# Four instead of eight output tiles of the heads' projection cut along the depth, and fewer PSUM banks for scores and transposes

## The chip, the core and the metric

The kernel runs on one core of one Trainium2 chip. The metric is the device time of one execution, in microseconds; several runs are given by their median. The engines are PE (TensorE, with its weight loads as PEld), DVE (VectorE), ACT (ScalarE), POOL (GpSimd) and SP, which issues the DMAs.

## What is computed

The program is two blocks of two layers each on a sequence of 512 tokens of width 1024. The first block is not touched. In the second block each layer computes, in the terms of the reference:

```python
y_pool = pool_mixer(u, pool_w, pool_scale)
y_nsa = nsa_mixer(q, kv[:, :, 0], kv[:, :, 1], gates, q_norm, k_norm, cmp_pe, cmp_w1, cmp_w2)
mix = jnp.concatenate([y_pool, y_nsa], axis=-1) @ w_out
x = x + gate1 * mix
h2 = rms_norm(x, norm2) * (1.0 + scale2) + shift2
ff = jnp.square(jax.nn.relu(h2 @ w_ff1)) @ w_ff2
return x + gate2 * ff
```

`nsa_mixer` has eight heads of width 64, each with two masked softmax attentions over the 512 tokens and one over compressed tokens. Rows 512 to 1023 of `w_out` belong to the heads; this product is "the heads' projection".

## The kernel before

Activations lie transposed, 128 features by 512 tokens to a tile; x is eight such tiles, m = 0 to 7. Each operand of a matmul is split into a high and a low part, and `mm3` (line 406 issues each matmul) multiplies high by high, high by low and low by high. A weight "unit" is 512 KB: one DMA into `wraw`, a rounding on ACT into `wH` (line 452) and a subtraction on DVE into `wL` (line 453); three units fit at a time (`wH2`, `wL2`).

In the second block `main2` makes the projections of a layer, and `weave` steps the heads (`nsa_prep`, `nsa`), the compressed attention and the pooling between them. `nsa` runs 16 steps, eight heads with two attentions b = 0, 1 each. A step has two stages, and `two_stage` runs the second stage of one step beside the first of the next:

- first stage, four row blocks of 128 queries: scores on PE into a tile S of PSUM; line 710 on DVE reads S, adds the mask, takes the smallest of the negated scores and writes `p` to SBUF; line 711 on ACT takes the exponential with its sum. Then lines 1759 and 1760 (DVE) make the factors, and line 1764 (POOL, blocks of 128 and 256) and 1766 (DVE, blocks of 384 and 512) scale `p`.
- second stage, four column blocks: transposes on PE (line 415) into a tile M of PSUM, a rounding on ACT (line 419) and a subtraction on DVE (line 420) which both read M; then the product with the values, accumulated over both attentions of a head in one tile M that stays open until line 1792 (ACT) and line 1794 (DVE) have read it. After each second head a 128-wide tile of `yn` is split by lines 419 and 420.

The heads' projection contracts over the four tiles k of `yn`. A matmul result is accumulated in a tile of PSUM and added into x by line 1507 on DVE. Before, the depth is cut in two: a unit `o2h` holds k = 0, 1 or k = 2, 3 of four output tiles. After the flag `yn1` (heads 0 to 3 done) `quad_unit` adds k = 0, 1 of all eight x tiles; after `yn` it adds k = 2, 3 of tiles 0 to 3, and `in_halves` makes a generator that `turn` runs later for k = 2, 3 of tiles 4 to 7, first for tokens 0 to 255, then for tokens 256 to 511. `turn` also makes the sum of squares (lines 650 to 661), its norm (`stat_half`: line 657 adds, ones-matmuls, a power on POOL, a broadcast by matmul) for each half, and `h2` (lines 1347 to 1349), whose result feeds the first three units of the feed-forward product.

The order of all instructions on each engine is not written by hand: a list scheduler places them, and each takes its turn when its operands and a buffer are there. PSUM has eight banks of 128x512 f32, and every PSUM tile takes one. `CAPS` gives for each tag how many tiles may be open at once: in the second block S2 (scores) 3, M2 (all else of the attention) 5, accn2 (projections beside the heads) 2, acc2 (those of `turn` and of the projections before) 7; the eight banks are shared among them.

## Time and profile before

| | |
|---|---|
| median of three runs | 2393.4 us (2393.25 to 2394.74) |
| the profiled execution's own time | 2391.33 us |
| its span | 2389.5 us |
| busy: PE, DVE, ACT, POOL | 98%, 69%, 44%, 11% |
| granted clock of TensorE, mean | 0.994 of 2.4 GHz |

A busy time is the union of an engine's instructions; matmuls are pipelined, so that PE counts as busy also when it could issue faster. The second block's heads run from about 1304 to 1419 us of the span in its first layer, and from 1898 to 2012 us in its second. The windows view gives busy times of a stretch, the timeline gives each instruction, and the waits say what ended an engine's idle time.

### The profile page before, as it was taken

Reading aid. Unit: us, or ns where it says so; the run is one execution under the profiler, and the core shown is the slowest. Engines: PE = TensorE matmul, PEld = TensorE weight load, DVE = VectorE, ACT = ScalarE, POOL = GpSimd, SP = SyncE. Lnnn points to the kernel's source line nnn. Section 1 sums busy time; section 2 is a strip of 40 time slices with the busy share of each in tenths; the row PEclk is TensorE's granted clock in tenths of the full one; section 3 lists DMA queues with packets and bytes.
Section 4 is the critical chain, followed back from the end, with each engine's and each line's share of the span. In section 5 each row is a group of like instructions: output and inputs, shape, how many; then the busy total and the mean of one; then the engine's idle time right before and its main releaser. Section 6 shows DMA issues by size and latency. Waiting matters only on the chain.

```text
span 2389.5 us, 31476 instructions
## 1 busy us (share of the span) xinstructions
PE 2342.3 (98%) x11684; PEld 1973.3 (83%) x11684; DVE 1640.2 (69%) x3410; ACT 1048.7 (44%) x1930; POOL 264.3 (11%) x254
## 2 busy tenths in 40 slices
PE   8999999999999999999999989999999998999999
PEld 7888888888888888888888778888888876888888
DVE  5679975567588987656579886666647988644342
ACT  6455543434446554343246654332324665433231
POOL 0011010000001001000055310000005531000000
PEclk9999999999999999999999999999999999999999
DMA  5222222245543222225332013555523211223222
GB/s 173 88 80 71 80 80 97 82 156 205 182 159 115 71 80 80 97 88 172 126 102 80 27 37 104 193 194 194 193 97 105 68 35 37 80 94 100 98 93 84
DMA packets 87851, 256.62 MB, mean 107 GB/s; under 512 B 9745, under 2 KB 10769, under 8 KB 87697
## 3 DMA queue, kind: packets, MB, share of 16 engines
q1 hardware_dynamic: 87552, 254.45, 31.9%
q8 instruction: 92, 1.51, 0.3%
q14 instruction: 63, 0.51, 0.1%
q10 hardware_dynamic: 144, 0.15, 0.0%
HBM read 250.37 MB, written 4.19 MB: 107 GB/s over the span
## 4 chain that ended last, share of the span: by engine, by line
PE 93%; DVE 5%; ACT 1%; issue 1%; DMA 0%; POOL 0%; DVEq 0%; ACTq 0%; POOLq 0%
PE acc L406 78%; PE M L406 5%; PE accn L406 4%; PE S L406 3%; PE M L415 3%; DVE p L420 1%; DVE p L710 1%; DVE b L1507 1%; DVE wL L453 1%; ACT p L419 0%; DVE p L1766 0%; ACT p L711 0%; DVE tmp_s L1794 0%; DMA wraw<-wp_in 0%; ACT tmp_s L1792 0%
## 5 line engine op out<-in xcount | busy, mean ns | idle before, releaser
L406 PE MATMUL acc<-h,wH 128*128 128x512 f32 (+2 forms) x2944 | 872.6, 380 | 9.5 <-ACT h L423 7.3
L452 ACT CAST wH<-wraw 128x1024 fp32r<-128x1024 f32 x358 | 375.2, 1051 | 656.8 <-PE acc L406 400.0
L406 PEld LDWEIGHTS acc<-h,wH 128*128 128x128 f32 (+1 forms) x2944 | 537.4, 189 | 106.1 <-ACT h L423 7.3
L453 DVE TENSOR_TENSOR wL<-wraw,wH 128x1024 fp32r<-128x1024 f32 x358 | 437.5, 1223 | 164.9 <-ACT wH L452 156.9
L406 PE MATMUL acc<-h,wL 128*128 128x512 f32 (+1 forms) x1440 | 546.2, 380 | 0.0
L406 PE MATMUL acc<-b,wH 128*128 128x512 f32 (+1 forms) x1696 | 503.9, 374 | 0.0
L406 PEld LDWEIGHTS acc<-b,wH 128*128 128x128 f32 x1696 | 311.8, 189 | 56.3
L406 PEld LDWEIGHTS acc<-h,wL 128*128 128x128 f32 x1440 | 272.7, 190 | 49.6
L406 PE MATMUL acc<-wH,h 128*128 128x512 f32 (+1 forms) x1024 | 310.0, 380 | 0.0
L406 PE MATMUL acc<-b,wL 128*128 128x512 f32 (+1 forms) x784 | 291.5, 372 | 0.0
L406 PEld LDWEIGHTS acc<-wH,h 128*128 128x128 f32 x1024 | 187.2, 188 | 33.7
L406 PE MATMUL acc<-wL,h 128*128 128x512 f32 (+1 forms) x512 | 194.7, 380 | 0.0
L1390 DVE SCALAR_TENSOR_TENSOR b<-acc,keep,b 128x512 f32<-128x512 f32 (+1 forms) x68 | 48.9, 720 | 183.9 <-PE acc L406 183.5
L406 PEld LDWEIGHTS acc<-b,wL 128*128 128x128 f32 x784 | 147.9, 189 | 25.4
L711 ACT ACTIVATE p<-p,nb 128x128 f32<-128x128 f32 x192 | 107.9, 564 | 77.7 <-DVE nb L710 76.7
L1325 DVE SCALAR_TENSOR_TENSOR keep<-keep 128x512 f32<-128x512 f32 x192 | 126.0, 686 | 11.1 <-DMA keep<-w_mod_in 10.9
L578 POOL TENSOR_TENSOR sm_bs<-sm_as,keep 128x4 f32<-128x4 f32 (+1 forms) x48 | 65.7, 1376 | 413.4 <-DVE sm_as L574 374.1
L406 PEld LDWEIGHTS acc<-wL,h 128*128 128x128 f32 x512 | 96.5, 188 | 16.2
L406 PE MATMUL S<-b,b 128*128 128x128 f32 (+3 forms) x480 | 108.9, 338 | 0.1
L710 DVE CUSTOM_DVE_ANT_0 p<-S,keep 128x128 f32<-128x128 f32 x192 | 101.3, 542 | 4.9 <-PE S L406 3.6
L415 PE MATMUL M<-keep,p 128*128 128x128 f32 x608 | 97.4, 275 | 2.7 <-DVE tmp_s L1794 1.0
L406 PE MATMUL M<-p,b 128*128 128x256 f32 (+3 forms) x352 | 81.7, 323 | 10.3 <-DVE p L420 9.0
(294 smaller groups left out, 2898.8 us busy)
## 6 DMA issues: line engine op xcount, KB each, us to landing
wraw<-wp_in SPq DMA_DIRECT2D x364, 512.0 KB, 3.5
keep<-w_mod_in SPq DMA_DIRECT2D x192, 256.0 KB, 3.6
b<-x_in SPq DMA_DIRECT2D x8, 256.0 KB, 6.3
g<-x_in SPq DMA_DIRECT2D x8, 256.0 KB, 4.4
x_spill<-tmp_m SPq DMA_DIRECT2D x8, 256.0 KB, 3.9
g<-x_spill SPq DMA_DIRECT2D x8, 256.0 KB, 3.8
out<-b SPq DMA_DIRECT2D x6, 256.0 KB, 2.0
keep<-parq_in SPq DMA_DIRECT2D x2, 384.0 KB, 6.9
```

Of the source, the lines that this page charges most:

```text
L406: return self.nc.tensor.matmul(out, l, r, start=start, stop=stop)
L415: self.nc.tensor.transpose(out, in_, self.ident[:n, :n])
L420: return self.nc.vector.tensor_sub(l, src, fbits(h))
L452: self.cut_h = nc.scalar.copy(h, raw)
L453: self.cut = nc.vector.tensor_sub(l, raw, fbits(h))
L578: self.pow = nc.gpsimd.tensor_tensor(r[:p, :n], m[:p, :n], self.mhalf[:p, :n], ALU.pow)
L710: nc.vector.tensor_tensor_reduce(p, s, mask, nscale, 3e38, ALU.add, ALU.min, accum_out=nb)
L711: nc.scalar.activation(p, p, AF.Exp, bias=nb, scale=-1.0, accum_out=accum)
L1325: nc.vector.scalar_tensor_tensor(w, w, 1.0, crow[:, T * k:T * k + T], ALU.mult, ALU.mult, accum_out=ms[:, 2 * f + k:2 * f + k + 1])
L1390: nc.vector.scalar_tensor_tensor(x(m)[:, ts], ps[:, ts], mt[:, 40 + m:41 + m], x(m)[:, ts], ALU.mult, ALU.add)
L1507: nc.vector.scalar_tensor_tensor(x(m)[:, ts], ps[:, ts], mt[:, 16 + m:17 + m], x(m)[:, ts], ALU.mult, ALU.add)
```

## The change

`quad_unit` on k = 0, 1 is now called for tiles 0 to 3 alone (`range(1)`). Tiles 4 to 7 no longer have a cut depth: the generator of `in_halves` is made of two units `o2`, each with all four k of two tiles, and computes tokens 0 to 255 and then 256 to 511 of these tiles over k = 0 to 3. `in_halves` loses its offset `k0`. The caps S2 and M2 go from 3 and 5 to 2 and 4.

```diff
-    def in_halves(self, jobs, src, use, k0=0):
+    def in_halves(self, jobs, src, use):
...
-        for mq in range(2):
+        for mq in range(1):
             for i, _ in enumerate(self.quad_unit(("o2h", l, 0, mq), S["yn"], 0, 4 * mq, use)):
...
         yield from self.quad_unit(("o2h", l, 1, 0), S["yn"], 2, 0, use2)
-        S["emit"] = self.in_halves([(("o2h", l, 1, 1), [4, 5, 6, 7])], S["yn"], use2, 2)
+        S["emit"] = self.in_halves([(("o2", l, 1, mp), [2 * mp, 2 * mp + 1]) for mp in range(2, 4)], S["yn"], use2)
...
-        "acc2": 7, "accn2": 2, "S2": 3, "M2": 5, "b82": 10, "tmp_m2": 3, "tmp_s2": 5, "tmp_c2": 5, "tmp_p2": 4, "wH2": 3, "wL2": 3}
+        "acc2": 7, "accn2": 2, "S2": 2, "M2": 4, "b82": 10, "tmp_m2": 3, "tmp_s2": 5, "tmp_c2": 5, "tmp_p2": 4, "wH2": 3, "wL2": 3}
```

The number of weight units stays (four to a layer). Per layer, 24 matmuls of 128x512 become 48 of 128x256, and the accumulations of line 1507 that stand beside the heads go from sixteen to twelve (eight of them are the pooling's part): those of k = 0, 1 on tiles 4 to 7 are gone.

The scheduler then places the work anew from the start of the second block's heads on. The names below carry the numbers of tiles: S2 scores, M2 transposes or head sums, p42 and p22 the attention weights, acc2 and accn2 projections. The places are those of the second block's first layer; the second layer reads alike.

The first place is PE at the start of the last step (head 7, b = 1), before:

```order
L406 MATMUL S2_2551_12777<-b82_2146_11252,b82_2066_10865 128x512 x2
L406 MATMUL S2_2565_12833<-b82_2147_11253,b82_2066_10865 128x128 x2
L406 MATMUL S2_2571_12849<-b82_2147_11253,b82_2066_10865 128x256 x2
L406 MATMUL M2_2535_12726<-p42_2521_12662,b42_2139_11197 128x384
L406 MATMUL M2_2535_12726<-p22_2519_12660,b42_2139_11197 128x256
L415 MATMUL M2_2547_12760<-keep1_1_61,p22_2515_12652 128x128
L415 MATMUL M2_2547_12760<-keep1_1_61,p42_2514_12651 128x128 x2
L406 MATMUL M2_2535_12726<-p22_2519_12660,b42_2139_11197 128x256
L406 MATMUL M2_2535_12726<-p42_2520_12661,b42_2139_11197 128x128
L415 MATMUL M2_2550_12772<-keep1_1_61,p42_2514_12651 128x128 x2
L406 MATMUL M2_2535_12726<-p42_2521_12662,b42_2139_11197 128x128
L415 MATMUL M2_2553_12783<-keep1_1_61,p42_2514_12651 128x128
```

and in the change:

```order
L406 MATMUL S2_2560_12811<-b82_2147_11253,b82_2066_10865 128x128 x2
L406 MATMUL M2_2535_12726<-p42_2543_12746,b42_2140_11198 128x128
L406 MATMUL M2_2535_12726<-b82_2132_11167,b42_2110_11022 128x512 x2
L415 MATMUL M2_2565_12820<-keep1_1_61,p42_2536_12735 128x128
L415 MATMUL M2_2565_12820<-keep1_1_61,p22_2537_12736 128x128
L415 MATMUL M2_2565_12820<-keep1_1_61,p42_2536_12735 128x128 x2
L406 MATMUL S2_2566_12827<-b82_2147_11253,b82_2066_10865 128x256 x2
L415 MATMUL M2_2568_12833<-keep1_1_61,p22_2537_12736 128x128
L415 MATMUL M2_2568_12833<-keep1_1_61,p42_2536_12735 128x128 x2
L406 MATMUL S2_2569_12839<-b82_2147_11253,b82_2066_10865 128x384 x2
L415 MATMUL M2_2571_12845<-keep1_1_61,p42_2536_12735 128x128 x2
L406 MATMUL S2_2572_12850<-b82_2147_11253,b82_2066_10865 128x512 x2
```

Before, score matmuls of the last step (S2_2565, S2_2571) stand ahead of three of the transposes of the step two before it (M2_2547, M2_2550, M2_2553), and the last of them (S2_2577) stands ahead of all transposes M2_2570 of the step before. In the change the four scores of the last step (S2_2560 to S2_2572) alternate with the transposes of the step before it (M2_2565, M2_2568, M2_2571).

The second place is PE at the transposes of the last step, with the engines that each row waits for, before (M2_2585 to M2_2588; M2_2581 is the head's sum):

```order
L415 MATMUL M2_2585_12901<-keep1_1_61,p42_2562_12830 128x128 [waits PE_49,Pool_49]
L415 MATMUL M2_2585_12901<-keep1_1_61,p22_2563_12831 128x128 [waits Pool_49]
L415 MATMUL M2_2585_12901<-keep1_1_61,p42_2562_12830 128x128 x2
L406 MATMUL M2_2581_12889<-p22_2567_12839,b42_2139_11197 128x256 [waits DVE_49]
L406 MATMUL M2_2581_12889<-p42_2568_12840,b42_2139_11197 128x128 [waits Activation_49]
L415 MATMUL M2_2586_12908<-keep1_1_61,p22_2563_12831 128x128 [waits PE_49]
L415 MATMUL M2_2586_12908<-keep1_1_61,p42_2562_12830 128x128 x2
L406 MATMUL M2_2581_12889<-p42_2569_12841,b42_2139_11197 128x128 [waits DVE_49]
L415 MATMUL M2_2587_12914<-keep1_1_61,p42_2562_12830 128x128 x2
L406 MATMUL M2_2581_12889<-p42_2583_12899,b42_2140_11198 128x512 [waits Activation_49]
L415 MATMUL M2_2588_12919<-keep1_1_61,p42_2562_12830 128x128 [waits DVE_49]
L406 MATMUL M2_2581_12889<-p42_2584_12900,b42_2140_11198 128x512
```

and in the change (M2_2580 to M2_2583; M2_2576 is the head's sum):

```order
L415 MATMUL M2_2580_12879<-keep1_1_61,p42_2557_12808 128x128 [waits Pool_49]
L415 MATMUL M2_2580_12879<-keep1_1_61,p22_2558_12809 128x128 [waits Pool_49]
L415 MATMUL M2_2580_12879<-keep1_1_61,p42_2557_12808 128x128 [waits DVE_49] x2
L406 MATMUL M2_2576_12867<-p42_2578_12877,b42_2140_11198 128x512 [waits Activation_49]
L415 MATMUL M2_2581_12886<-keep1_1_61,p22_2558_12809 128x128 [waits DVE_49]
L415 MATMUL M2_2581_12886<-keep1_1_61,p42_2557_12808 128x128 x2
L406 MATMUL M2_2576_12867<-p42_2579_12878,b42_2140_11198 128x512
L406 MATMUL M2_2576_12867<-p42_2578_12877,b42_2140_11198 128x384 [waits Activation_49]
L415 MATMUL M2_2582_12892<-keep1_1_61,p42_2557_12808 128x128 [waits DVE_49]
L415 MATMUL M2_2582_12892<-keep1_1_61,p42_2557_12808 128x128
L406 MATMUL M2_2576_12867<-p42_2579_12878,b42_2140_11198 128x384
```

Each of the transposes M2_2581 and M2_2582 now waits for DVE, as M2_2583 does; before, only the last one did. The built program's list of tiles says which bank each has: before, M2_2585 to M2_2588 lie in banks 0, 7, 2, 0. In the change M2_2580 to M2_2583 all lie in bank 6, the transposes M2_2544, M2_2547, M2_2550, M2_2553 of the step two before in banks 4, 7, 4, 7, and M2_2565, M2_2568, M2_2571, M2_2574 with the scores S2_2560, S2_2566, S2_2569, S2_2572 in 7, 4, 7, 6 and 4, 4, 6, 4. The four acc2 tiles of the generator take banks 0 and 5 during the fifth head and also 3 and 2 during the sixth, and keep them to the end; before, three opened (in banks 6, 5, 1) right after the last score and the fourth (2) during the last head's sum.

The third place is DVE in the norm after the heads, before:

```order
L453 TENSOR_TENSOR wL2_2651_13218<-wraw_2649_13215,wH2_2650_13217 128x1024
L1507 SCALAR_TENSOR_TENSOR b82_1977_10262<-acc2_2610_13013,keep1_1_61,b82_1977_10262 128x256
L661 TENSOR_TENSOR keep1_1_61<-keep1_1_61,tmp_m2_2599_12988 128x512
L1507 SCALAR_TENSOR_TENSOR b82_1977_10262<-acc2_2611_13014,keep1_1_61,b82_1977_10262 128x256
L1507 SCALAR_TENSOR_TENSOR b82_1977_10262<-acc2_2612_13015,keep1_1_61,b82_1977_10262 128x256
L453 TENSOR_TENSOR wL2_2655_13249<-wraw_2653_13246,wH2_2654_13248 128x1024
L661 TENSOR_TENSOR keep1_1_61<-keep1_1_61,tmp_m2_2601_12999 128x512
L657 TENSOR_TENSOR keep1_1_61<-keep1_1_61,tmp_m2_2613_13023 128x256
L657 TENSOR_TENSOR keep1_1_61<-keep1_1_61,tmp_m2_2614_13033 128x256
L657 TENSOR_TENSOR keep1_1_61<-keep1_1_61,tmp_m2_2615_13043 128x256
```

and in the change:

```order
L453 TENSOR_TENSOR wL2_2647_13234<-wraw_2645_13231,wH2_2646_13233 128x1024
L1507 SCALAR_TENSOR_TENSOR b82_1977_10262<-acc2_2609_13014,keep1_1_61,b82_1977_10262 128x256
L657 TENSOR_TENSOR keep1_1_61<-keep1_1_61,tmp_m2_2604_12989 128x256
L1507 SCALAR_TENSOR_TENSOR b82_1977_10262<-acc2_2610_13015,keep1_1_61,b82_1977_10262 128x256
L657 TENSOR_TENSOR keep1_1_61<-keep1_1_61,tmp_m2_2605_13005 128x256
L453 TENSOR_TENSOR wL2_2651_13265<-wraw_2649_13262,wH2_2650_13264 128x1024
L657 TENSOR_TENSOR keep1_1_61<-keep1_1_61,tmp_m2_2611_13029 128x256
```

Line 657 adds the squares of tiles 4, 5 and 6 for the first half of the tokens. Before, two weight splits of line 453 stand between the last head and these additions (wL2_2651 and wL2_2655, both in the piece); in the change three do (wL2_2643 stands five rows ahead of the piece), and the third, wL2_2651, stands just ahead of the third addition.

## Rows read from the trace of the kernel before

**Rows 1.** The page's part 4, the chain that ended last, by engine

```profile
PE 93%; DVE 5%; ACT 1%; issue 1%; DMA 0%; POOL 0%; DVEq 0%; ACTq 0%; POOLq 0%
```

**Rows 2.** Windows: length, busy (x count) of PE, PEld, DVE, ACT, POOL, PEclk, DMA share, GB/s

```profile
1304.30:1402.40 98.10, 90.75 (x506) 74.12 (x505) 89.24 (x247) 65.02 (x178) 31.66 (x39) 1.00 0.10 33
1402.40:1418.60 16.20, 14.08 (x81) 11.44 (x80) 12.11 (x33) 8.86 (x24) 3.84 (x4) 1.00 0.10 33
...
1430.20:1434.80 4.60, 0.02 (x1) 0.00 (x0) 4.36 (x9) 3.14 (x8) 0.00 (x0) 0.89 0.60 180
1434.80:1444.00 9.20, 7.87 (x35) 7.71 (x36) 5.74 (x17) 3.10 (x7) 1.58 (x2) 0.50 0.06 24
...
1996.00:2012.20 16.20, 14.04 (x81) 11.42 (x80) 12.08 (x33) 8.81 (x24) 3.84 (x4) 1.00 0.10 33
```

**Rows 3.** Waits of DVE, 1304.3 to 1418.6 (total us, times, longest)

```profile
DVE b L1507 <- PE accn L406: 4.3, 5, 2.0
```

**Rows 4.** Groups by line and form, DVE, 1304.3 to 1418.6 (xcount | busy, mean ns | idle)

```profile
L1507 DVE SCALAR_TENSOR_TENSOR b<-accn,keep,b 128x512 f32<-128x512 f32 x16 | 11.8, 744 | 4.3 <-PE accn L406 4.3
L453 DVE TENSOR_TENSOR wL<-wraw,wH 128x1024 fp32r<-128x1024 f32 x7 | 8.5, 1218 | 0.0
```

**Rows 5.** Timeline of DVE from the seventh head's second transposes (start, length, what)

```profile
1402.40 0.69 DVE L420 TENSOR_TENSOR p<-M,p 128x512 fp32r<-128x512 f32 x1 [0.59 <-ACT p L419]
1403.01 0.34 DVE L710 CUSTOM_DVE_ANT_0 p<-S,keep 128x128 f32<-128x128 f32 x1
...
1403.28 0.48 DVE L710 CUSTOM_DVE_ANT_0 p<-S,keep 128x256 f32<-128x256 f32 x1
...
1404.22 0.55 DVE L420 TENSOR_TENSOR p<-M,p 128x384 fp32r<-128x384 f32 x1
...
1404.78 0.59 DVE L420 TENSOR_TENSOR p<-M,p 128x256 fp32r<-128x256 f32 x2
...
1406.02 1.04 DVE L1766 TENSOR_SCALAR p<-p,rsum 128x384 f32<-128x384 f32 x2
1406.98 0.74 DVE L710 CUSTOM_DVE_ANT_0 p<-S,keep 128x512 f32<-128x512 f32 x1
...
1409.44 0.17 DVE L1759 RECIPROCAL rsum<-sum 128x4 f32<-128x4 f32 x1
```

**Rows 6.** Timeline of PE, last scores and last head's transposes

```profile
1405.04 0.62 PE L406 MATMUL S<-b,b 128*128 128x512 f32 x2
...
1413.06 0.60 PE L415 MATMUL M<-keep,p 128*128 128x128 f32 x4
...
1413.67 0.51 PE L415 MATMUL M<-keep,p 128*128 128x128 f32 x3
...
1414.08 0.40 PE L415 MATMUL M<-keep,p 128*128 128x128 f32 x2
...
1415.06 0.33 PE L415 MATMUL M<-keep,p 128*128 128x128 f32 x1 [0.23 <-DVE p L420]
...
1415.92 0.63 PE L406 MATMUL accn<-b,wH 128*128 128x512 f32 x2
```

**Rows 7.** Timeline of ACT, the last exponential and the last head's evictions

```profile
1407.78 0.71 ACT L711 ACTIVATE p<-p,nb 128x512 f32<-128x512 f32 x1
...
1413.69 1.28 ACT L419 CAST p<-M 128x512 fp32r<-128x512 f32 x3 [1.91 <-PE M L415]
1415.42 0.27 ACT L419 CAST p<-M 128x128 fp32r<-128x128 f32 x1 [0.45 <-PE M L415]
```

**Rows 8.** Timeline of POOL, the last head's scaling

```profile
1409.98 2.16 POOL L1764 TENSOR_SCALAR p<-p,rsum 128x128 f32<-128x128 f32 x2 [2.67 <-ACT tmp_s L1792]
```

**Rows 9.** Timeline of DVE, the last head's end

```profile
1414.31 1.70 DVE L420 TENSOR_TENSOR p<-M,p 128x512 fp32r<-128x512 f32 x4 [1.37 <-ACT p L419]
1418.59 0.68 DVE L1794 TENSOR_TENSOR tmp_s<-M,tmp_s 64x512 f32<-64x512 f32 x1 [2.58 <-ACT tmp_s L1792]
```

**Rows 10.** Timeline of PE, the first matmul of the norm after the heads

```profile
1434.82 0.58 PE L406 MATMUL M<-keep 128*128 128x1 f32 x2 [4.59 <-DVE keep L657]
```

More of the change, by code (lines that the diff above doesn't have):

```diff
@@ L491, in emit @@
                     for k in range(nk):
-                        mm = self.products(ps[a][:, ts], h, l, a * nk + k, src.h(k0 + k, ts), src.l(k0 + k, ts), k == 0, k == nk - 1)
+                        mm = self.products(ps[a][:, ts], h, l, a * nk + k, src.h(k, ts), src.l(k, ts), k == 0, k == nk - 1)
                         if k == nk - 1:
@@ L1904 @@
 NLAST = 2
-NLASTP = 2
 SLOTS = (1, 3)
```

## Prediction

> **What bounds the kernel now.** I read the chain of waits first. PE carries 93% of it [rows 1], so in most of the program only PE work counts. The change leaves that part alone: the orders of the engines differ from the second block's heads on, and after the heads the feed-forward products stand as before but for their start. So I read the windows of the heads [rows 2]. From the first transposes of the heads to the second transposes of the seventh head is 98.1 us, with DVE busy 89.2 and PE 90.8; the last part, to the last head's sum, is 16.2 us. Both layers read alike to 0.1 us, so I work out one layer and double it. Here no engine is full: DVE, PE and ACT hand tiles to each other through PSUM. The largest wait of DVE is for PE's projection matmuls, 4.3 us [rows 3]. Behind the heads lies a third stretch, the norm: PE has nothing for 4.6 us, waits for line 657, and then runs 9.2 us at a granted 0.50 of its clock, the 1.2 GHz level [rows 2, 10].
>
> The sums go against the profiled execution, 2391.33 us with a span of 2389.5; the median of the runs is 2393.4, 2.1 above it, and I add the difference to that. No change, for a measurement of this kernel, is within 0.2%, 4.8 us.
>
> **The change part by part, for one layer.**
>
> *Work removed.* Four accumulations of line 1507 at 0.744 us [rows 4] go from DVE: 3.0 us. On PE, 24 matmuls of 512 columns become 48 of 256, the same columns, of which half move behind the last head into the 4.6 us where PE stands idle. Units, DMAs and roundings are the same in number, so SP and POOL have nothing new; the two kinds of unit are 512 KB each. If all that work lay on the path, 3.0 us would be the gain.
>
> *First part, 98.1 us.* Counted in the order, DVE has two accumulations fewer here (twelve for fourteen), one weight split fewer (five for six) and one pair of line 1766 more: 2 x 0.744 + 1.218 - 1.04 = 1.7 us less [rows 4, 5]. The other half of the removed accumulations, 1.5 us, and one split stood in the last part. Against this, PE issues eight more projection matmuls of 512 columns ahead of the first transposes, and the four tiles acc2 of the generator hold two banks from the fifth head and four from the sixth. From there on scores, transposes, sums and accn2 share four banks, where before they had eight. Bounds: if the 1.7 us count and the 4.3 us of waits for the projection vanish, -6.0; if each of the four steps with two banks for transposes pays half of what I find below for one bank (half of 2.4, so 1.2), and PE's early matmuls come on top with about 1.0, +5.8. I take 0, the middle: DVE's work and PE's are nearly the same, and which engine waits is only shuffled.
>
> *Last part, 16.2 us: scores against transposes.* Before, line 420 on the seventh head's second transposes starts at 1402.40, and line 1759 of the last step at 1409.44 [rows 5]: 7.0 us, with DVE full, two accumulations and a split in it. The last scores had been computed early (the last one at 1405.04 [rows 6]) because their banks were free. In the change these scores alternate with the eighth head's first transposes in banks 4, 7 and 6. Each must wait until the tile before it in its bank has been read. I follow the chain in rows. DVE first does 0.69 + 0.17 + 0.17 + 0.55 + 1.04 + 0.59 = 3.2 us (lines 420, 1759, 1760, 420, 1766, 420) until bank 4 is clear [rows 5]. Then: first score about 0.3, line 710 0.34, head sum and transposes about 0.9, second score 0.3, line 710 0.48, transposes 0.51, eviction on ACT about 0.5, line 420 0.55, last score 0.62, line 710 0.74, exponential 0.71 with its sum 0.2 [rows 5 to 7]: 6.15 us. Twelve hand-overs at about 0.05 (the transposes that end at 1413.66 are taken up by ACT at 1413.69 [rows 6, 7]) add 0.6. Together 9.95 for 7.0: **+2.9**. Bounds: 0, if the scheduler's order happens to leave DVE full; +4, if DVE's other rows come late as well.
>
> *Last part: the last head's transposes.* Before, the four groups lie in four banks and flow: from 1413.06 to the end of the last line 420 at 1416.01 is 2.95 us [rows 6, 9]. In the change all four lie in bank 6, and each row waits for DVE to have read the one before. Then the lengths add: PE 0.60 + 0.51 + 0.40 + 0.33 = 1.84, ACT 1.28 + 0.27 = 1.55, DVE 1.70, and eight hand-overs of 0.04: 5.4 us, 2.4 more [rows 6, 7, 9]. Some comes back. Before, the transposes started 0.9 us after POOL had scaled the blocks (1412.14 [rows 8]), because products of the step before stood ahead of them and waited; in the change these can be done in time. Before, three projection matmuls also stood between the last products, from 1415.92 on with 0.63 for the first two [rows 6], about 0.8 us in all, that in the change have been done. So 2.4 - 0.9 - 0.8 = **+0.7**. Bounds: -1.0 (if the lengths overlap as before) and +2.4.
>
> Here a sentence of the Trainium skill speaks against me. The page "TensorE: Matmul & The Clock Gate", section "HAM oscillation — how this bites in real kernels", reports that adding PSUM double-buffering gave no further gain in one kernel. By it the loss of banks would cost nothing and the sum of the last part would be the removed work alone; no run here has shown that for these steps, and the four-bank flow of the last head in the rows is where I find it unlikely.
>
> *The norm behind the heads.* The accumulations on DVE are the same. But the two units `o2` stay in use until the generator's end, so that a third split of line 453, 1.218 us [rows 4], stands between them and the third line 657, which PE waits for: **+1.2**. PE's 24 extra matmuls of 256 columns lie in its 4.6 us of idle time and cost nothing; if that cover were gone they would cost at most 3.7 us (two of 512 columns take 0.62 [rows 6], so one of 256 at most 0.155). They shorten the gap to some 4.6 + 1.2 - 3.7 = 2.1 us or a little more. Before, PE fell to 0.50 after the gap of 4.6 us. If in the change it kept 2.4 GHz, half of its 9.2 us at the lower level, less what waits for POOL and DVE in it, some 3 us, would come back. I take no gain, because PE has little to do in all of this stretch. Bounds: -1.8 and +1.2.
>
> The same page, in its section "Loop structure matters more than you think", says that matmuls which follow immediately keep PE warm. By it the shorter gap would count, and this term would be -1.8 instead of +1.2.
>
> *Sum.* 0 + 2.9 + 0.7 + 1.2 = 4.8 us per layer, 9.6 for both. 2391.3 + 9.6 = 2400.9 for a profiled execution, **2403.0** as a median. The measurable change is thus +0.4%.
>
> **The rivals.**
>
> *Faster: the removed DVE work counts in full.* Place: DVE's queue through the heads. Price: 3.0 us per layer, 6.0 in all, so 2387.4. It decides if scores and transposes find their bank read before DVE has run out of other rows; then DVE stays as full as it is now (89.2 of 98.1) and simply has less to do. For it: four accumulations are really gone, and the 4.3 us of waits on them sit at the same place. Against it: in the last two heads DVE has no spare rows left, just there the accumulations were the filler. Chance 0.17.
>
> *No change.* The bank waits cost about what the removed work saves, 3.0 per layer, or the caps do nothing, since the eight banks were shared before and are shared now: 2393.4. For it: terms of both signs in every stretch. Chance 0.14, with the lowest outcomes of my forecast.
>
> *Slower by twice as much.* The shortage begins with the sixth head, where the generator takes its third and fourth bank: four steps at the 1.2 us above, 4.8 per layer on top of my sum, 2393.4 + 2 x 9.6 = 2412.6. For it: transposes there alternate between two banks. Against it: two banks can still be filled in turn, and DVE has 89.2 us of work to overlap. Chance 0.10.
>
> **How the numbers follow.** My forecast has 0.59, 2403.0, its own range 2397 to 2411. Slower by over 0.2% is the forecast with the third rival, 0.69; within 0.2%: 0.14; faster: 0.17. The range goes from 2388, which takes in most of the faster side's milder half, to 2414, past the third rival: some 0.1 is left out below and 0.05 above.
>
> **What would show it.** In the profile of the changed kernel: the last head's four transposes each start only after line 420 of the one before, and from the first to the last line 420's end it takes 5 us or more, not 2.95. From line 420 of the seventh head's second transposes to line 1794 of the last head it takes about 19.8 us, not 16.2. The first part stays near 98. Accumulations of line 1507 at 512 columns are 32 for 40 in all. The gap of PE ahead of the norm shrinks to 2 or 3 us, and the clock there stays at 0.50 for some 9 us. I am wrong if the last part is no longer than 16 us with the transposes still on one bank, or if the first part is shorter by more than 3 us; then DVE's relief has won.

## The result and the profile after

The changed kernel takes **2418.53 us** (median of 4 runs, 2417.68 to 2420.29) against 2393.32 for the kernel before beside it (4 runs, 2388.20 to 2394.74): ratio 1.0111, 95% interval 1.0099 to 1.0124. It is slower, and by 25.2 us, where 9.6 were forecast. The profiled execution took 2420.29 us, 29.0 more than that of before; its span is 2418.5 us.

The windows of the heads in the changed kernel, for the stretches of [rows 2] and with the same columns: first and last part of the first layer, PE's gap ahead of the norm, the 10 us behind it, and both parts of the second layer:

```profile
1306.90:1411.00 104.10, 93.17 (x517) 76.22 (x517) 89.86 (x253) 64.89 (x175) 32.74 (x40) 0.98 0.10 31
1411.00:1431.80 20.80, 15.44 (x62) 9.40 (x62) 10.76 (x29) 8.60 (x23) 3.50 (x4) 0.85 0.00 0
1447.50:1450.20 2.70, 0.09 (x2) 0.01 (x1) 2.64 (x6) 2.59 (x6) 0.00 (x0) 0.88 0.59 194
1450.20:1460.20 10.00, 8.91 (x41) 8.74 (x42) 6.70 (x19) 3.57 (x8) 1.50 (x2) 0.52 0.17 52
1916.90:2019.10 102.20, 92.46 (x518) 75.22 (x518) 89.25 (x250) 64.84 (x177) 31.58 (x40) 1.00 0.10 32
2019.10:2040.40 21.30, 15.76 (x62) 9.76 (x62) 10.83 (x30) 8.60 (x24) 3.50 (x4) 0.83 0.00 0
```

DVE is as busy in the first part as before (89.9 us for 89.2) but needs 104.1 us for it, not 98.1. The last part is 4.6 us longer with less work on DVE (10.8 for 12.1), and the granted clock is no longer 1.00 there. The first layer's ledger: the first transposes come 2.5 us later (line 420 at 1306.86, before 1304.32), the first part takes 6.0 us more, the last part 4.6, and from the last head's sum to PE's first matmul of the norm it takes 18.4 us, before 16.2: 15.4 in all. In the second layer the same four stretches add 3.6, 4.2, 5.0 and 1.5 us: 14.3.

In the first part DVE's waits grow from 7.7 to 12.6 us. Those for projection matmuls stay at 4.3 us [rows 3 for before]. New are those of line 710, 4.5 us; before, the same view has no row of it. Of the waits of DVE, 1306.9 to 1411:

```profile
DVE p L710 <- PE S L406: 1.9, 3, 0.9
DVE p L710 <- ACT p L419: 1.7, 1, 1.7
...
DVE p L710 <- PE M L406: 0.9, 1, 0.9
```

The timeline of DVE, for the stretch of [rows 5] and on to the last head, shows the alternation that was forecast:

```profile
1411.00 0.69 DVE L420 TENSOR_TENSOR p<-M,p 128x512 fp32r<-128x512 f32 x1 [0.76 <-ACT p L419]
...
1414.79 0.35 DVE L710 CUSTOM_DVE_ANT_0 p<-S,keep 128x128 f32<-128x128 f32 x1 [0.56 <-PE S L406]
...
1416.20 0.48 DVE L710 CUSTOM_DVE_ANT_0 p<-S,keep 128x256 f32<-128x256 f32 x1 [1.05 <-PE S L406]
...
1420.87 0.18 DVE L1759 RECIPROCAL rsum<-sum 128x4 f32<-128x4 f32 x1 [0.68 <-ACT p L711]
...
1424.51 0.69 DVE L420 TENSOR_TENSOR p<-M,p 128x512 fp32r<-128x512 f32 x1 [2.30 <-ACT p L419]
1426.36 0.56 DVE L420 TENSOR_TENSOR p<-M,p 128x384 fp32r<-128x384 f32 x1 [1.15 <-ACT p L419]
1428.10 0.42 DVE L420 TENSOR_TENSOR p<-M,p 128x256 fp32r<-128x256 f32 x1 [1.19 <-ACT p L419]
1429.39 0.29 DVE L420 TENSOR_TENSOR p<-M,p 128x128 fp32r<-128x128 f32 x1 [0.86 <-ACT p L419]
```

From line 420 at 1411.00 to line 1759 at 1420.87 it takes 9.87 us, and DVE waits for scores that came early before. The last head's transposes, one bank for all four, run as a chain, as PE's timeline shows too ([rows 6, 9] for before):

```profile
1425.26 0.55 PE L415 MATMUL M<-keep,p 128*128 128x128 f32 x3 [0.22 <-DVE p L420]
...
1426.97 0.69 PE L415 MATMUL M<-keep,p 128*128 128x128 f32 x2
...
1428.58 0.47 PE L415 MATMUL M<-keep,p 128*128 128x128 f32 x1
```

From the last group that POOL releases (1423.31) to the end of the last line 420 (1429.68) it takes 6.4 us; before it was 2.95. The chain of waits, from the projection to the norm, in time order (start, length, what):

```profile
1441.83 5.65 PE acc L406 x47
1447.47 0.02 issue
1447.50 1.05 ACT wH L452
1448.55 0.02 issue
1448.58 1.23 DVE wL L453
1449.80 0.35 DVE keep L657
1450.15 0.04 issue
1450.19 1.88 PE M L406 x8
```

The third split lies on the path, and ahead of it now ACT's rounding too, since the unit's buffer comes free only with PE's last projection matmul.

### The profile page after: what moved, and what is told of

Read it like the earlier page. It is cut to its first block, busy times and chain, and to the rows that moved or that the text cites. A ratio compares the mean times of both kernels' runs of the same rounds, so it can differ in the third digit from the quotient of the medians.

```text
span 2418.5 us, 31574 instructions
## 1 busy us (share of the span) xinstructions
PE 2361.4 (98%) x11732; PEld 1982.4 (82%) x11732; DVE 1639.9 (68%) x3402; ACT 1052.7 (44%) x1930; POOL 257.3 (11%) x254
## 4 chain that ended last, share of the span: by engine, by line
PE 91%; DVE 6%; ACT 1%; issue 1%; POOL 1%; DMA 1%; DVEq 0%; ACTq 0%; POOLq 0%
PE acc L406 76%; PE M L406 5%; PE accn L406 4%; PE S L406 4%; PE M L415 3%; DVE p L710 1%; DVE p L420 1%; DVE wL L453 1%; DVE p L1766 1%; DMA wraw<-wp_in 1%; DVE tmp_s L1794 0%; ACT p L419 0%; POOL sm_bs L578 0%; ACT p L711 0%; POOL p L1764 0%
## 5 line engine op out<-in xcount | busy, mean ns | idle before, releaser
L406 PE MATMUL acc<-b,wH 128*128 128x512 f32 (+1 forms) x1760 | 517.2, 372 | 0.0
L406 PEld LDWEIGHTS acc<-b,wH 128*128 128x128 f32 x1760 | 322.8, 190 | 56.5
L406 PE MATMUL acc<-b,wL 128*128 128x512 f32 (+1 forms) x816 | 301.2, 370 | 0.0
L406 PEld LDWEIGHTS acc<-b,wL 128*128 128x128 f32 x816 | 154.9, 190 | 25.5
L415 PE MATMUL M<-keep,p 128*128 128x128 f32 x608 | 105.4, 282 | 13.8 <-POOL p L1764 3.4
L710 DVE CUSTOM_DVE_ANT_0 p<-S,keep 128x128 f32<-128x128 f32 x192 | 102.3, 542 | 16.1 <-PE S L406 9.4
L406 PEld LDWEIGHTS acc<-wL,h 128*128 128x128 f32 x512 | 96.5, 188 | 16.2
L415 PEld LDWEIGHTS M<-keep,p 128*128 128x128 f32 x608 | 73.9, 143 | 38.1 <-DVE p L420 10.0
```

What stands on the lines that cost most here:

```text
L406: return self.nc.tensor.matmul(out, l, r, start=start, stop=stop)
L415: self.nc.tensor.transpose(out, in_, self.ident[:n, :n])
L710: nc.vector.tensor_tensor_reduce(p, s, mask, nscale, 3e38, ALU.add, ALU.min, accum_out=nb)
```

## The experiments

The computation is whole in all runs; they change the order or the caps. Where an edit moved the lines, the text keeps the numbers of the kernel before; in the rows of e10_lateT, L1766 on POOL is its line 1764. "Over before" is against the median of before beside that run (2390.5 to 2391.0 us). "Six heads" runs from the first line 420 of the heads to line 1794 of the sixth head, "two heads" on to that of the eighth, "norm" on to PE's first norm matmul, all in the first layer of the one profiled execution (the second layer can differ: in e16_b12_45 its six heads take 94.8 us and its two heads 25.1); the clock is that of the two heads, from the windows. The two runs with 4, 5 and 3, 6 carry the moved split of e12_before_split as well.

| run | caps S2, M2 | over before, us | six heads | two heads | clock | norm |
|---|---|---|---|---|---|---|
| before | 3, 5 | | 90.9 | 23.3 | 1.00 | 16.2 |
| the change | 2, 4 | +25.2 | 96.0 | 29.0 | 0.89 | 18.4 |
| e1_caps | 2, 4 | +40.6 | 100.3 | 30.9 | 0.76 | 16.3 |
| e7_s2 | 2, 5 | +24.6 | 96.9 | 26.9 | 0.88 | 17.1 |
| e8_m4 | 3, 4 | +18.6 | 95.5 | 23.2 | 0.86 | 17.1 |
| e14_fill12 | 2, 4 | +29.0 | 99.9 | 26.6 | 0.90 | 16.0 |
| e3_late | 2, 4 | +21.7 | 97.1 | 24.5 | 0.98 | 16.0 |
| e6_half | 2, 4 | +22.8 | 96.5 | 25.0 | 1.00 | 18.3 |
| e9_a25 | 2, 5 | +24.7 | 96.8 | 26.8 | 0.94 | 16.8 |
| r5_after13 | 2, 4 | +28.2 | 99.3 | 29.4 | 0.91 | 16.0 |
| e4_late35 | 3, 5 | +6.2 | 91.4 | 25.6 | 1.00 | 18.1 |
| e10_lateT | 3, 5 | +1.8 | 91.2 | 25.1 | 0.93 | 15.6 |
| e11_lateT_split | 3, 5 | -2.0 | 91.2 | 24.9 | 0.93 | 14.5 |
| e18_two | 3, 5 | -0.4 | 90.2 | 23.4 | 1.00 | 16.1 |
| e12_before_split | 3, 5 | +0.9 | 92.0 | 23.3 | 1.00 | 15.1 |
| e16_b12_45 | 4, 5 | +6.3 | 98.9 | 18.2 | 1.00 | 15.2 |
| e16_b12_36 | 3, 6 | +27.4 | 98.7 | 30.4 | 0.82 | 15.5 |
| r1_rate20 | 3, 5 | +25.5 | 93.9 | 26.6 | 0.91 | 16.2 |
| r2_rate13 | 3, 5 | +12.4 | 96.4 | 24.0 | 1.00 | 14.5 |
| r3_pool15 | 3, 5 | +13.0 | 93.5 | 26.7 | 0.88 | 17.1 |

### One part of the change at a time

The caps alone, on the kernel before (e1_caps):

```diff
-        "acc2": 7, "accn2": 2, "S2": 3, "M2": 5,
+        "acc2": 7, "accn2": 2, "S2": 2, "M2": 4,
```

> The kernel before with the two caps alone (S2 2, M2 4); the projection stays in two parts for all eight tiles. Theory A, the caps carry the early loss and the early opened tiles the late one: the first transposes' line 420 at 1306 to 1307 instead of 1304.3, the stretch to the seventh head's second transposes 101 to 104 us instead of 98.1, the last part 16 to 19 us, the median 2403 to 2412 us. Theory B, the banks that the generator's tiles hold from the fifth head on carry nearly all of it: this kernel opens them behind the last scores as before, so 2391 to 2398 us.

Measured 2431.24 us, ratio 1.0174 (1.0159 to 1.0189). The caps alone cost more than the whole change; the new projection gives 12.7 us back on top of them (15.4 if each kernel is set against the before beside it). My theory B falls, and theory A was still far too low.

The change with the generator's first half late (e3_late):

```diff
-                    self.mm(s[:, ks], q[:, qs], kT[b][:, g, 1, ks], False, True)
+                    self.last = self.mm(s[:, ks], q[:, qs], kT[b][:, g, 1, ks], False, True)
...
+                        with self.tc.issue_after(self.last.ins):
-                        mm = self.products(ps[a][:, ts], h, l, a * nk + k, src.h(k, ts), src.l(k, ts), k == 0, k == nk - 1)
+                            mm = self.products(ps[a][:, ts], h, l, a * nk + k, src.h(k, ts), src.l(k, ts), k == 0, k == nk - 1)
```

(`issue_after` places the instructions behind the named one on its engine; the condition that keeps it to the units `o2` is left out here.)

> The change, but PE takes the generator's matmuls for the first half only behind the last score matmul, so that its four tiles hold no bank before; caps 2 and 4 as in the change. Theory A: the early loss stays (first part 101 to 104 us), the last part comes back to 17 to 19 us, the norm keeps its 2 us: 2406 to 2413 us. Theory B: first part 98 to 99, last part 16 to 17: 2396 to 2401 us.

Measured 2412.37 us, 1.0089 (1.0074 to 1.0104): first part 103.9 us, last part 17.6, both as theory A has them; the norm, 16.0, did not keep its 2 us. The change lies 6.2 us above this run. The early opened tiles are what was taken away between the two, but the order differs as well. With these tiles late the first part is as long as in the change (104.1).

The same with caps 3 and 5 (e4_late35; the change's early generator with these caps was not tried, since eight banks don't hold it):

> As the run with the generator's matmuls behind the last score matmul, but with the caps 3 and 5 of the kernel before. Theory A: start at 1304.3, first part 96.5 to 98.5 us, last part 15 to 16.5, norm 2 us longer: 2390 to 2397 us, which is 12 to 20 us below the same kernel with caps 2 and 4. Theory B: the caps add nothing, so the two kernels differ by less than 5 us.

Measured 2396.85 us, 1.0025 (1.0014 to 1.0037), 15.5 below its neighbour: first part 98.7, as before, so the first part's loss comes with the caps or with the order that they bring. The last part, 18.4, missed theory A's 15 to 16.5: the last head's four transposes lie in one bank (6) here too, behind 5.6 us of the generator's matmuls.

Only the generator's second unit late (e6_half; the condition is `spec[3] == 3`):

> The change, but only the second unit of the generator (tiles 6 and 7) waits behind the last score matmul; tiles 4 and 5 hold two banks from the fifth head on, as in the change, and caps are 2 and 4. Theory A and B alike: of what the early opened tiles cost, between a third and two thirds stays, so a time between that of the change (2418.5 us) and that of the run with both units behind the last scores, with a last part of 17.5 to 20 us. If it is the third and fourth bank that decide (from the sixth head on), it lies within 3 us of the run with both units late.

Measured 2413.39 us, within 3 us of the run with both late, so that of the 6.2 us less than a third stays. If they are the price of banks, it is the third and fourth, held from the sixth head on, and not the first two. The three steps 15.5 (caps), 6.2 (early tiles) and 6.2 (projection with late generator, one bank at the end) add up to 27.9 us, the distance of the change from the before beside these runs (25.2 from its own). Each is a difference of two kernels whose orders differ too.

### Which cap, and whether it is scarcity

On the kernel before, each cap by itself (e7_s2 and e8_m4: one number of the diff above):

> The kernel before with the cap of scores alone lowered (S2 2, M2 5). Both caps together cost 40 us. Theory S, DVE runs out of scores that are ready: most of it is here, 2415 to 2431 us, with the first part of the heads 103 to 107 us. Theory M, the four tiles for transposes and sums are what is short: 2391 to 2401 us, and the cost appears with M2 4. If each is harmless alone and only both together bind, both single runs lie under 2401 us.

> The kernel before with the cap of transposes and sums alone lowered (S2 3, M2 4). Theory M: 2415 to 2431 us, first part 103 to 107 us and a last part of 18 us or more. Theory S: 2391 to 2401 us.

2415.58 us (1.0099, 1.0084 to 1.0114) and 2409.60 us (1.0076, 1.0061 to 1.0091). Neither theory alone holds: S2 costs 24.6, M2 18.6, together 40.6. M2 4 alone came out below its range. Its two layers, which the scheduler laid in different orders, take 135.8 and 143.9 us from the first transposes to the norm: 8 us apart with the same caps and the same work.

What the tight caps do to the order is plain in the groups of PE's projection matmuls, accn (xcount | busy, mean ns | idle). Of before, 1348 to 1372, then 1404.3 to 1418.6:

```profile
L406 PE MATMUL accn<-b,wH 128*128 128x512 f32 x32 | 10.0, 394 | 0.0
L406 PE MATMUL accn<-b,wL 128*128 128x512 f32 x17 | 6.7, 395 | 0.0
...
L406 PE MATMUL accn<-b,wH 128*128 128x512 f32 x10 | 3.2, 400 | 0.0
...
L406 PE MATMUL accn<-b,wL 128*128 128x512 f32 x6 | 2.4, 392 | 0.0
```

Of the run with both caps, 1355 to 1379:

```profile
L406 PE MATMUL accn<-b,wH 128*128 128x512 f32 x44 | 14.3, 398 | 0.0
L406 PE MATMUL accn<-b,wL 128*128 128x512 f32 x21 | 8.3, 395 | 0.0
```

The windows of its first part, last part and last head:

```profile
1305.80:1412.90 107.10, 96.52 (x517) 78.25 (x517) 94.87 (x262) 66.06 (x178) 33.87 (x41) 0.98 0.11 35
1412.90:1437.00 24.10, 18.24 (x63) 11.82 (x62) 9.69 (x26) 8.30 (x21) 2.96 (x4) 0.69 0.00 0
1421.30:1437.00 15.70, 11.36 (x40) 7.01 (x38) 6.24 (x18) 5.53 (x14) 1.81 (x2) 0.72 0.00 0
```

and that of the last head before:

```profile
1409.90:1418.60 8.70, 6.80 (x44) 5.43 (x42) 4.73 (x12) 3.54 (x9) 2.16 (x2) 1.00 0.19 61
```

65 projection matmuls for 49 in 24 us in the middle. Before, 16 stood in the last 14.3 us of the heads; here the last begins at 1410.09, 26.9 us ahead of their end. So my reading was that the first part grows by the work drawn into it (DVE 94.9 us busy for 89.2), and the last heads are left with bare steps: 24.1 us with 9.7 of DVE, at a granted 0.69, and the last head alone 15.7 us for 8.7. To test that, 24 of these matmuls were held back (e14_fill12):

```diff
-        for mq in range(2):
-            for i, _ in enumerate(self.quad_unit(("o2h", l, 0, mq), S["yn"], 0, 4 * mq, use)):
+        for i, _ in enumerate(self.quad_unit(("o2h", l, 0, 0), S["yn"], 0, 0, use)):
...
+        for _ in self.quad_unit(("o2h", l, 0, 1), S["yn"], 0, 4, use, self.mark[12, 0]):
+            pass
```

(The last argument places its matmuls on PE behind the first score of the seventh head; this second loop stands behind `yn`.)

> The kernel before with caps 2 and 4 (2431.2 us), but the second unit of k = 0, 1 (24 projection matmuls of 512 columns for tiles 4 to 7) kept on PE behind the first score of the seventh head's first attention, so that the last heads again have projection work between their steps. Theory, the loss with fewer tiles is that projection work goes into the middle heads (51 and 39 of such matmuls in the fourth and fifth eighth of the heads' stretch, 32 and 27 before) and the last heads run bare: 2415 to 2425 us, last two heads 27 to 31 us instead of 36.7. Rival, the loss is the hand-over from tile to tile in each step, whatever stands between: 2428 to 2436 us.

Measured 2419.87 us: 11.4 us back with the same caps and the same work, two heads in 26.6 us at 0.90 instead of 30.9 at 0.76 (the 36.7 in the expectation is a slip; its rows give 30.9). The time is where the filler theory has it, and a quarter of the loss. The trace does not bear out its picture, though. The 24 matmuls stand from 1392.23 to 1399.5, in the sixth head, since PE computes scores ahead of the step that uses them. In the last two heads stand 6 projection matmuls, as in e1_caps. That the place of these matmuls is worth 11.4 us is shown; that they fill the last heads is not.

More tiles instead of fewer (e16_b12_45, e16_b12_36), on before with one weight split moved (below):

> The kernel before with that split moved and one tile more for scores (S2 4, M2 5). Lowering S2 from 3 to 2 cost 24.6 us. Theory, scores are short at 3 too: 3 to 10 us less than with 3. Rival, 3 is enough and the eight banks that all share are what limits next: within 3 us of its neighbour, or slower since scores then take banks from transposes.

> The kernel before with that split moved and one tile more for transposes and sums (S2 3, M2 6). Lowering M2 from 5 to 4 cost 18.6 us. Theory, five are short too: 3 to 10 us less. Rival, five are enough: within 3 us of its neighbour, or slower.

2397.12 us (1.0028, 1.0016 to 1.0039) and 2418.21 us (1.0112, 1.0096 to 1.0127). **One more tile for transposes costs as much as one less for scores.** Few tiles cannot be the reason there. So I changed the order and left the caps (r2_rate13 as shown; r1_rate20 with 2.0; r3_pool15 with RATEP 1.5 for 2.0 instead):

```diff
-RATE2 = 1.6
+RATE2 = 1.3
```

> The kernel before with caps 3 and 5 and all work as before; only the pace at which the heads' steps are handed to the scheduler beside the projections is lower (RATE2 1.3 for 1.6), so that the order of the engines changes and no tile is taken away. Theory scarcity, too few open tiles cost the time: within 6 us of before, 2385 to 2397 us. Theory order, any order but the one before costs 15 to 30 us, and the caps matter only since they change it: 2405 to 2420 us.

> The same with a higher pace (RATE2 2.0). 24 more projection matmuls then stand in the heads' second step and 24 each in the 13th to 15th, but 2 in the last. Theory scarcity: 2385 to 2397 us. Theory order: 2405 to 2420 us.

> The kernel before with a lower pace of the pooling alone (RATEP 1.5 for 2.0). The order of PE is that of before up to the eighth step; behind it projection matmuls go 24, 24, 24, 0, 24, 0 to the last six steps instead of 48, 12, 16, 14, 0, 18. Theory scarcity: 2387 to 2396 us. Theory order, and the filler of the last step decides: 2397 to 2410 us, with a last part of over 18 us.

2402.91 (1.0051, 1.0036 to 1.0066), 2416.01 (1.0110, 1.0095 to 1.0125) and 2403.49 us (1.0054, 1.0037 to 1.0070). All three lie outside what scarcity allows. The second and third are where the order theory has them, the first falls between the two. Filler in the last heads does not sort these runs either: before has 18 projection matmuls in the last two heads and takes 23.3 us, the runs with the higher pace and with the lower pace of the pooling have 28 each and take 26.6 and 26.7, the run with M2 6 has 9 and takes 30.4.

What these three share with the change is the end of the heads. There the last head's four line 420 again run as a chain. Of r1_rate20:

```profile
1422.25 0.69 DVE L420 TENSOR_TENSOR p<-M,p 128x512 fp32r<-128x512 f32 x1 [2.29 <-ACT p L419]
...
1427.13 0.29 DVE L420 TENSOR_TENSOR p<-M,p 128x128 fp32r<-128x128 f32 x1 [0.86 <-ACT p L419]
```

From the first to the end of the last it is 5.2 us here, 5.4 in r3_pool15 and 4.9 in e16_b12_36, as in the change (5.2) and in every run with S2 2 or M2 4 (4.8 to 5.5); in before and in r2_rate13 it is 1.7. The built programs put the last head's transposes into one bank in all three (7, 7 and 6). So the chain that I had put down to the caps comes with an order, also where no tile is missing. Its length differs by 3.1 to 3.7 us per layer from before; the rest of what these three runs lose is not located.

On the change itself, another order (r5_after13) and one more tile (e9_a25):

> The change itself (caps 2 and 4, generator early) with the lower pace (RATE2 1.3). Theory scarcity: the tiles are as few as in the change, so 2412 to 2425 us. Theory order: the time may go either way by 10 us or more, 2395 to 2440 us, and a time under 2405 us would show that caps 2 and 4 alone do not bind.

> The change with M2 at 5 again (S2 2, M2 5). On the kernel before, M2 4 alone cost 18.6 us. Theory scarcity: most of that comes back here, 2400 to 2408 us. Theory order: the order is another again, and the time anywhere from 2405 to 2435 us; above 2415 us one more tile would have given nothing.

2418.72 us and 2415.43 us: neither moves it by more than 3.1 us. A tile more does not give the cost back, and this one other order doesn't either.

### The last head, its bank and the clock

The generator behind the last head's transposes (e10_lateT: `self.last` set by the transposes instead of the scores; caps 3 and 5), and the same with the third split moved (e11_lateT_split; `self.added` is the third line 657):

```diff
+            behind = self.tc.issue_after(self.added.ins) if spec[:2] == ("s", "w_ff1_2") and spec[3] == 2 * P else ExitStack()
+            with behind:
-            self.cut = nc.vector.tensor_sub(l, raw, fbits(h))
+                self.cut = nc.vector.tensor_sub(l, raw, fbits(h))
```

> The change with the caps 3 and 5 of the kernel before, and the generator's first half behind the last head's transposes instead of the last scores, so that these four transposes have four banks (5, 0, 1, 6) again. In the run with the generator behind the last scores they lay in one bank and took 4.8 us from the first to the last line 420, and PE took 5.6 us of the generator's matmuls ahead of them. Theory, single bank and queue: from the first of these transposes to the end of the last line 420 3 us, last part 15 to 16.5 us instead of 18.4, the norm 18 to 19: 2390 to 2395 us. Rival, the bank does not matter because the lengths overlap anyway: within 2 us of 2396.9.

> As the run with the generator behind the last head's transposes, but with the third weight split of line 453 placed on DVE behind the third line 657 (for the third feed-forward unit alone). Theory, the split is on the path to PE's first matmul of the norm: 1.0 to 1.4 us less per layer there, 2 to 3 us less in all than its neighbour. Rival, DVE has slack there or the unit is then late for the product: within 1 us of its neighbour.

2392.84 us, 1.0004 (0.9994 to 1.0013), and 2389.00 us, 0.9995 (0.9985 to 1.0004). With four banks (5, 0, 1, 6) the four line 420 of the last head run through in 1.69 us; with one, in e4_late35, they took 4.8, and no projection matmul stood between its transposes either. The first and last of e4_late35, then all four of e10_lateT:

```profile
1415.83 0.69 DVE L420 TENSOR_TENSOR p<-M,p 128x512 fp32r<-128x512 f32 x1 [3.55 <-ACT p L419]
...
1420.31 0.29 DVE L420 TENSOR_TENSOR p<-M,p 128x128 fp32r<-128x128 f32 x1 [0.72 <-ACT p L419]
...
1414.82 1.69 DVE L420 TENSOR_TENSOR p<-M,p 128x512 fp32r<-128x512 f32 x4 [2.65 <-ACT p L419]
```

The last part is 17.8 us in the first layer, over the theory's 15 to 16.5, and 15.5 in the second. The norm did not grow to the 18 to 19 us expected: it is 15.6, with the clock at 0.99. PE idles 0.97 us behind the last head's sum, where in e4_late35 it idled 2.04 us and the norm had 0.81. The whole new projection with the old caps and a late generator is thus no measurable gain or loss: what the four accumulations save and what the rest costs cancel. The split shortens the norm from 15.57 to 14.49 us and from 15.33 to 14.41 in the second layer, 1.0 each, as expected; the median fell by 3.8, though the intervals overlap.

In the first of these runs both layers have the same order on PE up to and past the last head's transposes, and from 1405.88 (second layer 2001.14) the starts agree to 0.02 us until there. A timeline row of the first layer and of the second:

```profile
1413.27 2.18 PE L415 MATMUL M<-keep,p 128*128 128x128 f32 x9 [0.57 <-POOL p L1766]
...
2008.53 1.20 PE L415 MATMUL M<-keep,p 128*128 128x128 f32 x9 [0.57 <-POOL p L1766]
```

Two windows of the first layer, and the same two, 595.27 us later, of the second:

```profile
1410.00:1412.50 2.50, 1.24 (x8) 0.95 (x6) 2.10 (x7) 0.51 (x2) 1.13 (x2) 1.00 0.00 0
1412.50:1415.00 2.50, 1.93 (x9) 1.74 (x9) 0.18 (x1) 0.74 (x2) 0.71 (x1) 0.57 0.00 0
...
2005.27:2007.77 2.50, 1.24 (x8) 0.95 (x6) 2.09 (x7) 0.51 (x2) 1.11 (x2) 1.00 0.00 0
2007.77:2010.27 2.50, 1.93 (x16) 1.74 (x16) 0.54 (x1) 1.16 (x4) 0.71 (x1) 1.00 0.00 0
```

PE had been busy 1.24 us in both layers just ahead. In the first the clock then fell to the 1.2 GHz level (0.57 over the window), in the second it stayed at 2.4 GHz. The same nine transposes took 2.18 us and 1.20 us, and the last head 11.4 us and 9.1. Of these 2.3 us, 1.4 is the clock, by which the matmuls behind are late; the rest is the order of PE, which has eight more of the generator's matmuls ahead of the head's sum in the first layer.

Half of the generator ahead of the transposes, half behind (e18_two):

> As the run with the late generator and the moved weight split (2389.0 us), but the generator's first unit (tiles 4 and 5) goes behind the last score matmul and only the second behind the last head's transposes. In that run's first layer the granted clock was 0.93 in the last two heads and the last head took 11.3 us, 2 us more than the 9.1 of a layer at 1.00. Theory, the clock falls there since PE has nothing between the last head's steps, and a little work ahead of it keeps 2.4 GHz: last head 9 to 10 us in both layers, 2383 to 2388 us, faster than both kernels. Rival, the two tiles take banks from the last transposes, as all four did: last head 11 to 13 us, 2390 to 2396 us.

Measured 2390.36 us, 0.9999 (0.9990 to 1.0008). The last head takes 9.8 us at 1.00 in both layers, with transposes in banks 1, 6, 7, 1: the theory holds for the place. The time does not follow it, since the norm then takes 16.0 us at a granted 0.89 instead of 14.4 at 1.00. The generator's matmuls are done before the last head's sum, and PE idles 2.04 us behind it, 0.97 in e11_lateT_split. In this pair of runs the clock loses in the norm what it keeps in the last head.

And the moved split on the kernel before (e12_before_split):

> The kernel before, untouched but for the order on DVE of one weight split: that of the third feed-forward unit (line 453) goes behind the third line 657 of the first half. In the run with the change's projection, caps 3 and 5 and the generator late, the same edit shortened last head's sum to PE's first norm matmul by 1.0 us per layer. If that is the split alone and not the projection, 2 to 3 us less than before: 2387.5 to 2389.5 us. Rival, in the kernel before the split has slack: within 1 us.

Measured 2391.76 us, 1.0006 (0.9997 to 1.0015): no gain. The norm is shorter, 15.1 and 13.6 us for 16.2 (in the second layer also by the clock, 1.00 for 0.87), but the six heads take 92.0 and 93.2 us for 90.9. In the first layer that is not the split: DVE's order there is that of before, and the third head alone takes 1.05 us more (23.70 for 22.65), at a granted 0.93 for 1.00. In the second layer the order is another. So one profiled execution does not settle what the split alone is worth. No version beat both kernels measurably.

## Why the prediction was wrong in size

**Direction right, mechanism of the last part right.** Scores against transposes: 9.95 us worked out, 9.87 measured. That it fits to 0.1 us is in part luck: between the second and the last score the chain runs through DVE's own queue (lines 1794, 420, 710, 420), not through one eviction as I had it. Last head's transposes: 5.4 us worked out, and at least 5 named as the sign; 6.4 measured. Some 0.6 us of the excess lie in the sum, which added rows whose instructions overlap: DVE's 1.70 is 0.69 + 0.56 + 0.42 + 0.29 = 1.96 one by one, and there are more hand-overs than eight. Some 0.4 is the clock: at 1.00, in e4_late35, the same chain takes 6.0 us from the first transpose on (1414.58 to 1420.60). The last part: 19.8 worked out, 20.8 measured. Against me I had set the Trainium skill's page "TensorE: Matmul & The Clock Gate", section "HAM oscillation — how this bites in real kernels", by which more buffering in PSUM gave nothing in one kernel. Here it counts: with four banks for one, the last head's line 420 take 1.69 us in place of 4.8. The skill's page "Perfetto Trace Analysis", section "Matmuls", has it the way this trace does: independent groups should rotate through banks.

**The failed step: "First part ... I take 0".** It measured +6.0 us in the first layer, just past my upper bound of 5.8, and +4.2 in the second. "The first part stays near 98" failed with 104.1. The mechanism is not the one that made the bound. I had priced the banks that the generator holds from the fifth head on; with these tiles opened behind the last scores (e3_late) the first part still takes 103.9 us, and by the fourth head's sum (1374.99 for 1370.08) 4.9 us of the layer's 15.4 were lost, before any of these tiles was open. With caps 3 and 5 (e4_late35) it takes 98.7. My argument "DVE's work and PE's are nearly the same, and which engine waits is only shuffled" is what failed: DVE's work stayed (89.9 us for 89.2; the lines that I had counted as 1.7 us less are as counted, but a score block and rows of the compressed attention fall into the stretch as well), but its waits grew from 7.7 to 12.6 us, and 4.5 of them are line 710's, which had none. Also the same work with the same caps, in another order, cost 12.4 to 25.5 us on the kernel before. I had noted that the order is laid anew from the start of the heads on, and gave that no price. Of the first layer's 6.0, the third head has about 1.2 by the clock, as far as the layers can be compared: 17.2 us at a granted 0.90, 16.0 at 1.00 in the second layer.

**The missing term.** The stretch ahead of the first transposes had no term at all; it cost 2.5 us in the first layer and 3.6 in the second. Over both layers the first part makes 10.2 of the 20 us by which these stretches exceed my sum, the missing term 6.1; the last part and the norm, where I had terms, make 2.5 and 1.2.

**The caps.** A rival said that they "do nothing, since the eight banks were shared before and are shared now". A kernel with the lower caps takes 15.5 us more with the new projection and 40.6 with the old one. That is shown. How much of it is tiles that are short, and how much is only the order, is not: orders without a tile less cost 6 to 27 us, and the last head's chain in one bank stands in three of them too. So the larger part of the change's 25 us may be order, but no run had one order under both caps. That stays open.

**The norm.** +1.2 worked out, +2.1 measured. The split was priced rightly (1.0 by the run that moves it). The rest is PE, whose extra matmuls I had taken as free: its projection behind the heads now ends 15.7 us after the last head's sum (1431.82 to 1447.47), before 11.6, so that the gap is 2.7 us, as said (2 or 3), and the end of the projection releases the third unit, so that ACT's rounding lies on the path as well. Its clock there is 0.76, before 0.85; in e10_lateT, at 0.99, the norm with as many matmuls takes 15.6 us in all. PE stayed at 0.52 for 10 us behind the gap, as said.

**Removed work.** Line 1507 at 512 columns runs 32 times for 40, as counted. The new projection as a whole was worth nothing measurable with caps 3 and 5 and a late generator, and 12.7 us with caps 2 and 4 (15.4 against the befores beside each). What the removed accumulations alone are worth was not measured.

## What to carry to other kernels

Where a scheduler lays the order, a change of caps is a change of the whole order: measure it alone, against an order change that takes nothing away, before giving it a reason. In a stretch where no engine is full, the place of spare matmuls can be worth more than their own time: 24 of them placed later gave 11.4 us, though not at the place where I had expected it. Look in the built program which bank each of a loop's tiles has, and look at the end of the stretch first. When tiles of one loop share a bank, add their lengths, each instruction by itself, instead of overlapping them; for the last head's transposes the sum from merged rows came out 1.0 us short of 6.4.

## What the runs showed that I had not expected

One more tile for transposes (M2 6) made the kernel 27.4 us slower than before, as bad as one tile less for scores; its last head has the same chain in one bank. And the clock can differ between two layers that run the same instructions in the same order up to there: 0.57 against 1.00 over the same nine transposes, which cost 1.0 us on the spot. In the run with half of the generator late the last head gained by the clock, and the norm lost as much.
